# A fused transformer layer on one core: the first branch gated where it is evicted, a shift moved to DVE, a copy that scales, and scalar operands in a search

## The chip, the cores and the metric

One core of a Trainium2 chip runs the whole layer as one program. The metric is the device time of an execution in microseconds (us); a kernel's time is the median of its runs. The profile is that of one execution. Engines: PE (matrix products), DVE and POOL (elementwise work), ACT (elementwise work, functions and copies), SP (issues most transfers). Each engine runs its own instructions in order and waits on semaphores for the others.

## The reference, cut to what matters

```
hx = rms_norm(x) * (1 + sc1) + sh1                       # 1024 tokens, 1024 features
... projections of hx: recurrence branch xo, attention branch, and two gates xga, xgb (1024 features each)
a  = (rms_norm(xo) * silu(xg)) @ w_branch_a              # first branch
bb = attention_output @ w_branch_b                       # second branch
y  = (sigmoid(xga) * a + sigmoid(xgb) * bb) @ w_out      # merge, output projection
x  = x + g1 * y
h  = rms_norm(x) * (1 + sc2) + sh2                       # second norm
aff = softmax(h @ w_router)                              # 16 experts
gate, idx = top_k(aff.T, 128)                            # each expert takes its 128 best tokens
x  = x + g2 * sum over experts of gate * swiglu(h[idx])
out = rms_norm(x)
```

## The kernel before, in words

Each float32 product is made of three matmuls on parts with shorter mantissas (hi*hi, lo*hi, hi*lo; the helpers mm3 and mm3g, L176 to L178), so whatever becomes an operand of a product is split first: ACT writes the hi part (L92) and DVE the lo part (L93).

The program goes through these stages: normalisation and projections (to about 480 us), the recurrence (to about 640), attention (to about 1021), the merge (to about 1085), the output projection with the second norm and the router (to 1209), a search for the 16 thresholds (to about 1238), sixteen experts (1245 to about 1812) and the final norm.

During the recurrence and attention, matmuls of independent work ("fill") stand between the steps of the dependent chains. Part of it are the gate projections: `gate_proj(i, c)` makes gates i (0 for the first branch, 1 for the second), and each 128x512 block goes from PSUM (`pj`) through ACT into a tile `stg` and by a transfer to the DRAM buffer sGT (`staged`, L66). The last fill, `branch_a` (L873), multiplies the first branch by its weights: 16 blocks of 128x512, each copied by ACT from PSUM into a tile `stg` (a pool of three) and stored in sBA. It ends at 1021 us.

The merge has 16 steps, one for each 128x512 block (L978 to L1012). `gates` is called GA steps ahead: it loads both gate blocks from sGT into tiles `sgm`, ACT takes their sigmoids (L983), it loads the first branch's block from sBA into a tile `ba` and POOL multiplies it by the first gate (L987). The step itself is 12 matmuls of the second branch into PSUM `pb`, then three DVE instructions and one ACT copy: the second gate times `pb` (L1010, tile `sgm`), the sum (L1011, tile `ba`), and the split into the hi and lo parts `mg` (L92, L93).

The output projection (`py`) multiplies `mg` by the weights `wo`/`whi`, `wlo`. For each of 8 token tiles `y_part` adds the residual, takes the mean square, and from the norm's factor r (on POOL) it makes h: DVE multiplies x by r and s2 (L1090), POOL adds sh2 (L1091), and h is stored for the experts' gathers. PE transposes x1 (`pth`), multiplies by the router's weights (`plg`); `router` makes the softmax: DVE and ACT produce the exponentials `re`, DVE their reciprocal sum (L1113) and the affinities `aff` (L1114). `spread` repeats each affinity eight times with an ACT copy (`affb`, L1120), PE transposes that (`psp`, L1122), and two copies (`ar`) follow.

The search fixes the 128th largest affinity of each expert, three bits a round in ten rounds: DVE counts (`junk`, 128x1024, L1200 and L1202), writes a flag (`fl`), PE sums flags (`pn`), and DVE makes the next candidate from the count and an offset `bo`, which is the base plus a constant of its partition (L1214, L1217; both 128x1).

PE's order is fixed by the order in which the code emits it; the other engines' order is made by a scheduler from priorities (`tc.high_priority`). Transfers issued from SP are in one queue, in SP's order.

Of the kernel before, what the change touches and what calls it, by code (L numbers as in the profile page):

```python
# [9 lines left out]
F32 = mybir.dt.float32  # L10
# [18 lines left out]
def view(t, off, dims):  # L29
    """The tile's partitions with free dimensions [stride, size] from element off on."""  # L30
    a = t if isinstance(t, bass.AP) else t[:]
    return bass.AP(tensor=a.tensor, offset=a.offset + off, ap=[list(a.ap[0])] + [list(d) for d in dims])
# [13 lines left out]
def _layer(tc, nc, top, A, out):  # L46
# [35 lines left out]
    def rsqrt(pool, ss, n, scale, name):  # L82
        """(ss * scale + eps) ** -0.5"""
# [6 lines left out]
    def split(hi, lo, src, eng=None):  # L90
        """hi: src rounded to the parts' width; lo: what is left (exact)."""
        nc.scalar.copy(hi, src)  # L92
        (eng or nc.vector).tensor_tensor(lo, src, hi.bitcast(F32), op=OP.subtract)  # L93
# [3 lines left out]
    class Fill:  # L97
        """Matmuls of independent work, emitted between the steps of a dependent chain: the time is the tensor engine's."""
# [27 lines left out]
        def flushed(self):  # L126
            """The PSUM bank is on its way out: no matmuls into it for some steps."""
            self.wait = self.pause
# [7 lines left out]
    class Stream:  # L136
        """The weight chunks of the first sub-layer in the order of their use; each is loaded one chunk ahead."""
# [18 lines left out]
    def wload(src, kt, ncols, rowlen, off, hl=None):  # L156
        """A chunk of a weight: kt row tiles of 128, ncols columns from off on; as hi and lo."""
# [14 lines left out]
    def mm3g(p, a, b, nk, first=True, last=True):  # L172
        """p += sum over k of a[k].T @ b[k]; a, b: pairs of functions of k giving the hi and lo parts."""
# [15 lines left out]
    # the tokens, halves of them apart: [half][hi, lo]  # L189
# [15 lines left out]
    def natural(hi, lo, emit, tiles):  # L205
        """Token rows on the partitions: emit(token tile, PSUM); ctx tiles are 0, 1, x tiles 2 to 9."""
# [10 lines left out]
    def transposed(hi, lo, m, emit, ctx, halves=(0, 1)):  # L217
        """Features on the partitions: emit(first token, number of tokens, PSUM)."""
# [23 lines left out]
    with ExitStack() as st:  # L242
# [11 lines left out]
        # token tile t is loaded, normalised and transposed beside these row tiles of w_mod (9: after them)  # L254
# [51 lines left out]
        # rows 0, 1: the products with the hi parts of silu(c), silu(c_ctx); rows 2, 3: with the lo parts  # L306
# [64 lines left out]
    def rope_swap(o, x, s, eng):  # L371
        """o = x with the halves of each axis exchanged, times s; [128, heads, 64] each."""
# [4 lines left out]
    def gain_rows(rows, n):  # L377
        """A head's gains on all partitions, and the same with the halves of each axis exchanged."""
# [8 lines left out]
    lbp = consts.tile([128, 2, 4], F32, name="lbp")  # L387
    lb1 = consts.tile([128, 2, 4], F32, name="lb1")
    with ExitStack() as st:
        pool = st.enter_context(mkpool("right", name="sa", bufs=2))  # L390
        pps = st.enter_context(mkpool(name="saps", bufs=1, space=PSUM))
        # lower bounds: a softmax over the two layers' logits, its first component
# [19 lines left out]
        # keys: norm, rotary embedding; values as they are  # L412
# [63 lines left out]
        # the other adaLN parameters, as one row  # L476
# [33 lines left out]
        # their sums over the partitions, piece j of 512 on row j  # L510
# [20 lines left out]
    with ExitStack() as st:  # L531
# [27 lines left out]
        def gate_proj(i, c, halves=(0, 1)):  # L559
# [3 lines left out]
            for m in range(2):  # L563
                def emit(g, n, p):
                    staged(None, n, sGT[i, 2 * c + m, :, g - CT:g - CT + n], p)
# [7 lines left out]
        for i in range(2):  # L573
            for c in range(4):
                # of the last chunk the first half of the tokens first: it makes room
# [53 lines left out]
        def states(h, K, Z, acc, tt):  # L629
# [17 lines left out]
            def advance(d, i0, cs, kt):  # L647
# [3 lines left out]
                for i, c in enumerate(cs):  # L651
# [4 lines left out]
                    else:  # L656
                        # the state before the next chunk
# [60 lines left out]
    with ExitStack() as st:  # L718
# [131 lines left out]
        def branch_in():  # L850
            """The first half of the tokens makes room for the first branch's input."""
# [21 lines left out]
        def branch_a():  # L873
            for c in range(2):
                (w,), ahead = ws.next()
                ahead()
                for n in range(2):
                    for m in range(4):
                        p = pjt()
                        ts = slice(n * 512, n * 512 + 512)  # L880
                        yield from mm3g(p, (lambda k: w[0][:, k, m * 128:m * 128 + 128], lambda k: w[1][:, k, m * 128:m * 128 + 128]),
                                        (lambda k: BA[n][:, 0, k], lambda k: BA[n][:, 1, k]), 4)
                        staged(None, 512, sBA[4 * c + m, :, ts], p)
# [58 lines left out]
    with ExitStack() as st:  # L942
# [4 lines left out]
        # the router on x1: its weights take the norm's gain and the scale; the shift gives a row  # L947
# [21 lines left out]
        # merged branches: [hi, lo][row tiles 0-3, 4-7][tokens 0-511, 512-1023]  # L969
# [3 lines left out]
        with ExitStack() as st2:  # L973
            pool = st2.enter_context(mkpool("right", name="sg", bufs=1))
            steps = [(c, m, n) for c in range(2) for m in range(4) for n in range(2)]
            SG, GA = {}, 2

            def gates(c, m, n):  # L978
                SG[c, m, n] = []
                for b in range(2):  # L980
                    sgm = pool.tile([128, 512], F32, name="sgm", tag="sgm%d" % b, bufs=3)
                    nc.sync.dma_start(sgm, sGT[b, 4 * c + m, :, n * 512:n * 512 + 512])
                    nc.scalar.activation(sgm, sgm, AF.Sigmoid)  # L983
                    SG[c, m, n].append(sgm)
                x = stg.tile([128, 512], F32, name="ba", tag="stg")
                nc.sync.dma_start(x, sBA[4 * c + m, :, n * 512:n * 512 + 512])
                nc.gpsimd.tensor_tensor(x, x, SG[c, m, n][0], op=OP.mult)  # L987
                SG[c, m, n][0] = x
# [3 lines left out]
            for i, (c, m, n) in enumerate(steps):  # L992
# [17 lines left out]
                nc.vector.tensor_tensor(o[1], o[1], p, op=OP.mult)  # L1010
# [18 lines left out]
        nc.gpsimd.tensor_scalar(of16, offs[:, :4], 2.0 ** -16, None, op0=OP.mult)  # L1029
        iob = epc.tile([128, 128, 8], BF, name="iob")  # L1030
# [34 lines left out]
        def y_part(t, c, nc_):  # L1065
            """x1 = x + g1 * y, quarters c, ... of the columns; their part of the mean square."""
# [428 lines left out]
```

## Time and profile before

| | us |
|---|---|
| median of 3 runs | 1856.06 (1855.23 to 1858.42) |
| span of the profiled execution | 1854.5 |
| PE busy in the span | 1731.6 (93%) |
| DVE busy | 1331.0 (72%) |
| ACT busy | 995.4 (54%) |
| POOL busy | 273.7 (15%) |

The profile gives the span of its execution, from the first to the last instruction, and no time beside it; the median lies 1.6 us above that span. Busy shares are means over stages that have different limits.

### The profile page before, as it was taken

How to read it: one execution, taken by the hardware profiler on the slowest of the kernel's cores; microseconds unless marked ns; L12 is line 12 of the kernel's file. 1: busy time of each engine (PE TensorE's matmuls, PEld its weight loads, DVE VectorE, ACT ScalarE, POOL GpSimd, SP SyncE). 2: the span in 40 equal slices, each digit the busy share in tenths (PEclk: the TensorE clock that was granted, in tenths of full speed). 3: DMA queues.
4: the chain of work that ended last, by engine and by line, in shares of the span. 5: the costliest groups of instructions: out<-in, count | busy, mean ns of one | idle time of the engine just before them, and what ended most of it. 6: DMA issues, size and time to landing. Idle time of an engine off the chain costs nothing. (4 is left out here: it accounts for less than half of the span.)

```text
span 1854.5 us, 26192 instructions
## 1 busy us (share of the span) xinstructions
PE 1731.6 (93%) x9820; PEld 1454.9 (78%) x9820; DVE 1331.0 (72%) x2000; ACT 995.4 (54%) x1632; POOL 273.7 (15%) x241
## 2 busy tenths in 40 slices
PE   5899999999999799999999999939999999999995
PEld 2798887899988678787787788828888888887774
DVE  6656323876766466777875664469999999998897
ACT  6422331322323367777876532227777777777665
POOL 3400001020000201111100332140011001001103
PEclk9899999999999999999999999959999999999998
DMA  8285445353332410101212776459999999999972
GB/s 326 93 309 208 171 140 198 106 174 103 103 117 81 130 43 29 46 29 58 89 51 87 261 262 238 159 187 358 378 379 371 379 379 374 376 379 379 370 261 101
DMA packets 206319, 383.87 MB, mean 207 GB/s; under 512 B 17488, under 2 KB 65568, under 8 KB 202864
## 3 DMA queue, kind: packets, MB, share of 16 engines
q1 hardware_dynamic: 194944, 360.92, 54.4%
q0 software_dynamic: 4832, 19.34, 3.8%
q10 hardware_dynamic: 6416, 1.94, 0.4%
q8 instruction: 77, 1.26, 0.3%
q14 instruction: 50, 0.41, 0.1%
HBM read 323.02 MB, written 59.13 MB: 206 GB/s over the span
## 5 line engine op out<-in xcount | busy, mean ns | idle before, releaser
L93 DVE TENSOR_TENSOR elo<-eraw,ehi 128x1024 fp32r<-128x1024 f32 x378 | 452.2, 1221 | 22.2 <-ACT ehi L92 14.4
L92 ACT CAST ehi<-eraw 128x1024 fp32r<-128x1024 f32 x384 | 383.6, 1047 | 86.6 <-PE pgu L178 48.5
L177 PE MATMUL pgu<-elo,xeT 128*128 128x512 f32 x512 | 203.7, 398 | 2.8 <-DVE elo L93 2.4
L176 PE MATMUL pgu<-ehi,xeT 128*128 128x512 f32 x512 | 204.9, 400 | 0.2 <-ACT xeT L92 0.2
L178 PE MATMUL pgu<-ehi,xeT 128*128 128x512 f32 x512 | 202.4, 395 | 0.0
L176 PE MATMUL pj<-hx,whi 128*128 128x512 f32 x448 | 185.4, 414 | 6.5 <-ACT stg L69 5.3
L178 PE MATMUL pj<-hx,wlo 128*128 128x512 f32 x448 | 175.8, 392 | 0.0
L177 PE MATMUL pj<-hx,whi 128*128 128x512 f32 x448 | 175.5, 392 | 0.0
L795 ACT ACTIVATE p<-s,m,qsc 128x512 f32<-128x512 f32 (+1 forms) x192 | 134.3, 713 | 17.7 <-DVE m L792 17.5
L788 DVE TENSOR_REDUCE m<-s 128x1 f32<-128x512 f32 (+1 forms) x192 | 104.3, 596 | 48.5 <-PE s L786 48.2
L176 PE MATMUL pj<-whi,hx 128*128 128x256 f32 x448 | 130.9, 292 | 3.6 <-DVE stg L541 1.9
L92 ACT CAST pT<-ptp 128x512 fp32r<-128x512 f32 x160 | 92.7, 595 | 71.9 <-PE ptp L804 71.8
L178 PE MATMUL pj<-whi,hx 128*128 128x256 f32 x448 | 128.1, 286 | 1.4 <-DVE hx L93 1.3
L93 DVE TENSOR_TENSOR pT<-ptp,pT 128x512 fp32r<-128x512 f32 x160 | 108.3, 685 | 29.2 <-ACT pT L92 28.5
L177 PE MATMUL pj<-wlo,hx 128*128 128x256 f32 x448 | 127.4, 284 | 0.0
L177 PEld LDWEIGHTS pgu<-elo,xeT 128*128 128x128 f32 x512 | 96.3, 188 | 29.0 <-DVE elo L93 8.0
L176 PEld LDWEIGHTS pgu<-ehi,xeT 128*128 128x128 f32 x512 | 96.9, 189 | 21.8 <-ACT xeT L92 0.5
L178 PEld LDWEIGHTS pgu<-ehi,xeT 128*128 128x128 f32 x512 | 96.2, 188 | 22.6 <-DVE xeT L93 0.4
L1385 POOL DMA_INDIRECT ACC<-ye,idx x15 | 34.7, 2316 | 474.9 <-DVE ye L1384 474.9
L176 PE MATMUL pye<-ehi,hdT 128*128 128x512 f32 x256 | 104.8, 409 | 0.0
L177 PE MATMUL pye<-elo,hdT 128*128 128x512 f32 x256 | 102.1, 399 | 1.2 <-DVE elo L93 1.2
L814 PE MATMUL pv<-pT,vs 128*128 128x512 f32 x320 | 102.2, 403 | 0.9 <-DVE pT L93 0.8
(365 smaller groups left out, 3919.7 us busy)
## 6 DMA issues: line engine op xcount, KB each, us to landing
eraw<-in_w_exp_gate SPq DMA_DIRECT2D x64, 1024.0 KB, 12.0
eraw<-in_w_exp_up SPq DMA_DIRECT2D x64, 1024.0 KB, 11.6
eraw<-in_w_exp_down SPq DMA_DIRECT2D x64, 1024.0 KB, 12.2
wm<-in_w_mod SPq DMA_DIRECT2D x24, 1024.0 KB, 6.9
raw<-in_w_in SPq DMA_DIRECT2D x21, 1024.0 KB, 6.1
sFK<-sg SPq DMA_DIRECT2D x32, 256.0 KB, 2.3
sGT<-stg SPq DMA_DIRECT2D x32, 256.0 KB, 2.1
sgm<-sGT SPq DMA_DIRECT2D x32, 256.0 KB, 3.8
```

The source lines that it names most:

```text
L92: nc.scalar.copy(hi, src)
L93: (eng or nc.vector).tensor_tensor(lo, src, hi.bitcast(F32), op=OP.subtract)
L176: nc.tensor.matmul(p, a[0](k), b[0](k), start=s, stop=False)
L177: nc.tensor.matmul(p, a[0](k), b[1](k), start=False, stop=False)
L178: nc.tensor.matmul(p, a[1](k), b[0](k), start=False, stop=e)
L788: nc.vector.tensor_reduce(m[:, a:a + 1], s, axis=AX.X, op=OP.max)
L795: nc.scalar.activation(p, ss[a], AF.Exp, bias=m[:, 7:8], scale=sc, accum_out=SU[t, g][:, a, h:h + 1])
L814: nc.tensor.matmul(PV[t, g].rearrange("p a b -> p (a b)"), VS[:, g, j], hl[i], start=(j == 0 and i == 0), stop=(j == 9 and i == 1))
L1385: nc.gpsimd.indirect_dma_start(out=ACC, out_offset=bass.IndirectOffsetOnAxis(ap=idx[:, :1], axis=0), in_=ye, in_offset=None, compute_op=OP ...
```

## The change

1. `gate_proj` leaves PSUM through a sigmoid for the first branch's gates, so that sGT[0] holds sigmoids.
2. `branch_a` loads the block of gates into its tile (now `ga`) ahead of the matmuls, and DVE multiplies it by the product out of PSUM (L888 of the new kernel), in place of ACT's copy. sBA then holds the gated first branch.
3. `gates` of the merge loads one gate block, not two, and takes one sigmoid; POOL's multiplication is gone. It is called three steps ahead, not two, half of the `ba` tiles come from a pool of their own, and the DVE multiplication out of PSUM has a higher priority.
4. The second norm's `h + sh2` is on DVE; for the last tile it is emitted after `spread`.
5. The affinities' multiplication by the reciprocal sum is the scale of ACT's `affb` instruction; ACT then copies `aff` out of `affb`.
6. `bo` has one tensor and a scalar from a tile, where it had two tensors; a float32 copy of the offsets, `offf`, is made once on POOL.

The lines that differ besides are comments. The core of the diff:

```
@@ gate_proj
-                    staged(None, n, sGT[i, 2 * c + m, :, g - CT:g - CT + n], p)
+                    staged(None, n, sGT[i, 2 * c + m, :, g - CT:g - CT + n], p,
+                           None if i else lambda o, x: nc.scalar.activation(o, x, AF.Sigmoid))
@@ branch_a
+                        x = stg.tile([128, 512], F32, name="ga", tag="stg")
+                        nc.sync.dma_start(x, sGT[0, 4 * c + m, :, ts])
                         yield from mm3g(p, (lambda k: w[0][:, k, m * 128:m * 128 + 128], lambda k: w[1][:, k, m * 128:m * 128 + 128]),
                                         (lambda k: BA[n][:, 0, k], lambda k: BA[n][:, 1, k]), 4)
-                        staged(None, 512, sBA[4 * c + m, :, ts], p)
+                        with tc.high_priority(offset=SH[0]):
+                            nc.vector.tensor_tensor(x, x, p, op=OP.mult)
+                        nc.sync.dma_start(sBA[4 * c + m, :, ts], x)
@@ merge
-            SG, GA = {}, 2
+            SG, GA, HB = {}, 3, 40
             def gates(c, m, n):
-                SG[c, m, n] = []
-                for b in range(2):
-                    sgm = pool.tile([128, 512], F32, name="sgm", tag="sgm%d" % b, bufs=3)
-                    nc.sync.dma_start(sgm, sGT[b, 4 * c + m, :, n * 512:n * 512 + 512])
-                    nc.scalar.activation(sgm, sgm, AF.Sigmoid)
-                    SG[c, m, n].append(sgm)
-                x = stg.tile([128, 512], F32, name="ba", tag="stg")
+                sgm = pool.tile([128, 512], F32, name="sgm", tag="sgm", bufs=GA + 1)
+                nc.sync.dma_start(sgm, sGT[1, 4 * c + m, :, n * 512:n * 512 + 512])
+                nc.scalar.activation(sgm, sgm, AF.Sigmoid)
+                x = (stg.tile([128, 512], F32, name="ba", tag="stg") if n else
+                     pool.tile([128, 512], F32, name="ba", tag="ba", bufs=2))
                 nc.sync.dma_start(x, sBA[4 * c + m, :, n * 512:n * 512 + 512])
-                nc.gpsimd.tensor_tensor(x, x, SG[c, m, n][0], op=OP.mult)
-                SG[c, m, n][0] = x
+                SG[c, m, n] = x, sgm
...
-                nc.vector.tensor_tensor(o[1], o[1], p, op=OP.mult)
+                with tc.high_priority(offset=HB):
+                    nc.vector.tensor_tensor(o[1], o[1], p, op=OP.mult)
@@ second norm
-                h = pool.tile([128, D], F32, name="h", tag="h", bufs=1)
-                nc.vector.scalar_tensor_tensor(h, x1, r, row["s2"], op0=OP.mult, op1=OP.mult)
-                nc.gpsimd.tensor_tensor(h, h, row["sh2"], op=OP.add)
-                nc.sync.dma_start(H[ts], h)
+                if t < 7:
+                    second_norm(t, x1, r)
+
+        def second_norm(t, x1, r):
+            h = pool.tile([128, D], F32, name="h", tag="h", bufs=1)
+            nc.vector.scalar_tensor_tensor(h, x1, r, row["s2"], op0=OP.mult, op1=OP.mult)
+            nc.vector.tensor_tensor(h, h, row["sh2"], op=OP.add)
+            nc.sync.dma_start(H[t * 128:(t + 1) * 128], h)
@@ router, spread
-                nc.vector.tensor_scalar(aff[:, t], e, m[:, 3:4], None, op0=OP.mult)
+            EM[t] = e, m, x1, r
...
-                nc.scalar.copy(ab, aff[:, t, :, None].to_broadcast([128, 16, 8]))
+                e, m, x1, r = EM.pop(t)
+                nc.scalar.activation(ab, e[:, :, None].to_broadcast([128, 16, 8]), AF.Copy, scale=m[:, 3:4])
...
+                nc.scalar.copy(aff[:, t], ab[:, :, 0])
+            if t == 7:
+                second_norm(t, x1, r)
@@ search
-                        nc.vector.scalar_tensor_tensor(bo, base, 65536.0, offs[:, 4:5], op0=OP.mult, op1=OP.add)
+                        nc.vector.tensor_scalar(bo, base, 65536.0, offf[:, 4:5], op0=OP.mult, op1=OP.add)
...
-                        nc.vector.tensor_tensor(bo, base, (of16 if i < 3 else offs)[:, i + 1:i + 2], op=OP.add)
+                        nc.vector.tensor_scalar(bo, base, (of16 if i < 3 else offf)[:, i + 1:i + 2], None, op0=OP.add)
```

Three places show what moves. The first is DVE at the end of the merge, before; `wlo` is the last but one quarter of the output weights, and `sgm<-sgm,pb` is the multiplication out of PSUM.

```order
L1011 TENSOR_TENSOR ba<-ba,sgm 128x512
L93 TENSOR_TENSOR wlo<-raw,whi 128x2048
L93 TENSOR_TENSOR mg<-ba,mg 128x512
L1010 TENSOR_TENSOR sgm<-sgm,pb 128x512
L1011 TENSOR_TENSOR ba<-ba,sgm 128x512
L93 TENSOR_TENSOR mg<-ba,mg 128x512
```

The same place of DVE after the change:

```order
L1015 TENSOR_TENSOR ba<-ba,sgm 128x512
L93 TENSOR_TENSOR mg<-ba,mg 128x512
L1014 TENSOR_TENSOR sgm<-sgm,pb 128x512
L1015 TENSOR_TENSOR ba<-ba,sgm 128x512
L93 TENSOR_TENSOR wlo<-raw,whi 128x2048
L93 TENSOR_TENSOR mg<-ba,mg 128x512
```

The last multiplication out of PSUM stood behind `wlo` and a split; it now stands ahead of `wlo`.

The second place is DVE at a tile of the output projection (the seventh), before:

```order
L1111 TENSOR_SCALAR rm<-rm 128x1
L1090 SCALAR_TENSOR_TENSOR h<-x_11418,r_11514,s_10481 128x1024
L1113 RECIPROCAL rm<-rm 128x1
L1114 TENSOR_SCALAR aff<-re,rm 128x16
L1123 COPY ar_10443<-psp 128x128
```

The same place after the change:

```order
L1121 TENSOR_SCALAR rm<-rm 128x1
L1100 SCALAR_TENSOR_TENSOR h<-x_11371,r_11467,s_10435 128x1024
L1123 RECIPROCAL rm<-rm 128x1
L1101 TENSOR_TENSOR h<-h,sh_10433 128x1024
L1136 COPY ar_10395<-psp 128x128
```

`aff` is gone from DVE, and the addition of sh2 stands in its place, behind the reciprocal for which ACT waits.

The third place is SP, which issues the transfers, where `branch_a` ends and the merge begins, before:

```order
L868 DMA stg<-sOA 128x128
L70 DMA sBA<-stg 128x512 x4
L982 DMA sgm<-sGT 128x512
L70 DMA sBA<-stg 128x512
L982 DMA sgm<-sGT 128x512 x5
L70 DMA sBA<-stg 128x512 x2
L986 DMA ba<-sBA 128x512 x3
```

The same place after the change:

```order
L884 DMA ga<-sGT 128x512
L889 DMA sBA<-ga 128x512
L986 DMA sgm<-sGT 128x512
L990 DMA ba<-sBA 128x512
L986 DMA sgm<-sGT 128x512
L889 DMA sBA<-ga 128x512
L990 DMA ba<-sBA 128x512
L986 DMA sgm<-sGT 128x512
L889 DMA sBA<-ga 128x512
L990 DMA ba<-sBA 128x512
```

A load of gates now stands between the stores of `branch_a`, and the merge's first loads are three of each kind.

## Rows read from the trace of the kernel before

**Rows 1.** Windows by stage: length, busy time by engine, granted clock, DMA share, GB/s.

```profile
900.00:1021.00 121.00, 118.12 (x648) 96.37 (x647) 82.19 (x183) 89.59 (x204) 2.80 (x3) 1.00 0.22 75
1021.00:1090.00 69.00, 60.34 (x292) 50.71 (x291) 49.92 (x57) 36.46 (x53) 29.04 (x17) 0.93 0.76 252
1090.00:1210.00 120.00, 107.62 (x891) 105.69 (x891) 59.91 (x101) 24.90 (x76) 31.61 (x35) 0.97 0.59 211
1300.00:1500.00 200.00, 200.00 (x944) 162.15 (x943) 191.03 (x213) 150.33 (x168) 22.77 (x11) 1.00 1.05 377
```

**Rows 2.** Waits of PE, 1021 to 1210 us: total, times, longest.

```profile
PE psp L1122 <- ACT affb L1120: 10.1, 5, 2.9
PE py L176 <- DVE sgm L1010: 4.2, 1, 4.2
PE pb L176 <- DVE sgm L1010: 3.4, 1, 3.4
```

**Rows 3.** Timeline of PE in the merge: start, duration, instruction.

```profile
1054.75 0.39 PE L178 MATMUL pb<-br,wlo 128*128 128x512 f32 x1
1058.55 0.51 PE L176 MATMUL pb<-br,whi 128*128 128x512 f32 x1 [3.41 <-DVE sgm L1010]
...
1062.53 0.40 PE L177 MATMUL pb<-br,whi 128*128 128x512 f32 x1
...
1076.19 0.28 PE L176 MATMUL py<-wo,mg 128*128 128x256 f32 x1
...
1080.33 0.28 PE L178 MATMUL py<-whi,mg 128*128 128x256 f32 x1
1084.86 0.58 PE L176 MATMUL py<-wo,mg 128*128 128x256 f32 x1 [4.25 <-DVE sgm L1010]
...
1089.81 0.28 PE L178 MATMUL py<-whi,mg 128*128 128x256 f32 x1
```

**Rows 4.** Timeline of DVE at the end of the merge.

```profile
1080.26 2.28 DVE L93 TENSOR_TENSOR wlo<-raw,whi 128x2048 fp32r<-128x2048 f32 x1
1082.46 1.75 DVE L93 TENSOR_TENSOR mg<-ba,mg 128x512 fp32r<-128x512 f32 x1
```

**Rows 5.** Groups of instructions, 1021 to 1090 us: busy, mean ns.

```profile
L987 POOL TENSOR_TENSOR ba<-ba,sgm 128x512 f32<-128x512 f32 x16 | 28.9, 1813 | 120.8 <-ACT sgm L983 94.6 <-DMA ba<-sBA 26.1
...
L93 DVE TENSOR_TENSOR mg<-ba,mg 128x512 fp32r<-128x512 f32 x16 | 15.7, 991 | 4.7 <-ACT mg L92 4.3
L1011 DVE TENSOR_TENSOR ba<-ba,sgm 128x512 f32<-128x512 f32 x16 | 14.1, 889 | 2.8 <-POOL ba L987 2.7
...
L1010 DVE TENSOR_TENSOR sgm<-sgm,pb 128x512 f32<-128x512 f32 x16 | 10.7, 679 | 11.3 <-PE pb L178 7.2 <-ACT sgm L983 4.1
```

**Rows 6.** Timeline of POOL at the third tile and in the search.

```profile
1122.12 2.38 POOL L1091 TENSOR_TENSOR h<-h,sh 128x1024 f32<-128x1024 f32 x1 [1.40 <-DVE rm L1113]
...
1212.24 14.11 POOL L93 TENSOR_TENSOR elo<-eraw,ehi 128x1024 fp32r<-128x1024 f32 x6 [1.87 <-ACT ehi L92]
```

**Rows 7.** One line's instructions, L1114: shortest, median, longest ns.

```profile
L1114 DVE TENSOR_SCALAR aff<-re,rm x8: 234/1445/2378, 1122.2 to 1206.8; 128x16 f32<-128x16 f32 x8
```

**Rows 8.** Timeline of DVE in the search, where rounds begin with `junk`.

```profile
1209.25 1.28 DVE L1200 TENSOR_SCALAR_CACHE_REDUCE junk<-ar,of 128x1024 bf16<-128x1024 uint16 x1
...
1211.18 1.28 DVE L1200 TENSOR_SCALAR_CACHE_REDUCE junk<-ar,cand 128x1024 bf16<-128x1024 uint16 x1
...
1212.38 2.23 DVE L1217 TENSOR_TENSOR bo<-base,of 128x1 f32<-128x1 f32 x1
...
1219.26 0.14 DVE L1226 TENSOR_SCALAR bs<-base 128x1 f32<-128x1 f32 x1
...
1226.88 1.28 DVE L1202 TENSOR_SCALAR_CACHE_REDUCE junk<-ar,cand 128x1024 bf16<-128x1024 f32 x1
```

**Rows 9.** Groups of instructions of ACT, 900 to 1021 us.

```profile
L69 ACT COPY stg<-pj 128x512 f32<-128x512 f32 x16 | 9.4, 590 | 4.9 <-PE pj L178 4.5
```

**Rows 10.** Timeline of SP's queue at the last experts.

```profile
1763.19 9.86 SPq L1318 DMA_DIRECT2D eraw<-in_w_exp_down  x4
```

More of the change, by code (lines that the diff above doesn't have):

```diff
@@ L1029, in _layer @@
         nc.gpsimd.tensor_scalar(of16, offs[:, :4], 2.0 ** -16, None, op0=OP.mult)
+        offf = epc.tile([128, 10], F32, name="offf")
+        nc.gpsimd.tensor_copy(offf, offs)
         iob = epc.tile([128, 128, 8], BF, name="iob")
@@ L1101, in router @@
         def router(t):
-            _, _, _, hT, r = X1.pop(t)
+            _, x1, _, hT, r = X1.pop(t)
             p = ps.tile([128, 512], F32, name="plg", tag="pth")[:, :16]
@@ L1113, in router @@
                 nc.vector.reciprocal(m[:, 3:4], m[:, 2:3])
-                nc.vector.tensor_scalar(aff[:, t], e, m[:, 3:4], None, op0=OP.mult)
+            EM[t] = e, m, x1, r
+        EM = {}
         def spread(t):
```

## The prediction

> **What bounds the kernel now.** I read the page's busy shares first (PE 93% of the span), then windows cut by stage, then PE's waits in the stages where its share falls, and at those places the timelines of the engines that PE waited for. In attention PE is busy 118.1 of 121 us, in the experts all of 200 [rows 1]: nothing that only saves time on DVE, ACT or POOL can shorten these. In the merge it stands still for 8.7 of 69 us and in the output projection for 12.4 of 120 [rows 1], and it is there, and in the search behind them, that the change can pay. Three waits make up most of it: two on DVE's multiplication out of PSUM, and five on ACT's spread of the affinities [rows 2].
>
> **The merge (parts 1 to 3).** What the two stalls cost, from PE's timeline [rows 3]: at full clock the 35 matmul starts from 1076.19 to 1080.33 lie 0.118 us apart, and those of `pb`, with twice the columns, therefore about 0.236. The first stall is 1058.55 - 1054.75 less 0.24, that is 3.6 us; the eleven starts from 1058.55 to 1062.53 then take 3.98 us in place of 2.6, because after the pause the clock was granted at its lower level for a while (the stage's mean is 0.93 [rows 1]): another 1.4. The second is 1084.86 - 1080.33 less 0.12, that is 4.4 us, and its 23 starts up to 1089.81 take 4.95 us in place of 2.7: another 2.2. Together 11.6 us.
>
> Why DVE is late: 2.28 of `wlo` and 1.75 of a split stand ahead of the last multiplication [rows 4], 4.0 of the 4.4. The change's order puts that multiplication ahead of both. And the split is long: 991 ns on the mean and the sum 889 ns, where the multiplication out of PSUM, with as many elements, takes 679 [rows 5]. These two read two tiles of SBUF while POOL multiplies, and POOL's 16 instructions are 28.9 us long [rows 5]. Without them the 32 DVE instructions should fall to about 0.68 each: 15.7 + 14.1 - 21.8 = 8 us less. DVE's 49.9 us in the 69 [rows 1] become about 42; PE's work there, 60.3 less the 3.6 lost to the lower clock, is 57. DVE then has slack, and PE should bound the stage. The loads are 16 fewer of 48; the `ba` load stays and must still come back from a store, for which POOL waited 26.1 us [rows 5], now with one more step of lead and two more tiles. The bounds are 0 (the stalls come back through late loads) and 11.6; I take 11.6, since neither stall waited on a load at its end. Behind it, the last quarter of the output weights becomes the next thing to be late: its raw tile comes free only when `wlo` is done, which now follows the last block. By the present order of events I estimate a few microseconds of margin.
>
> **The price in attention (part 2).** ACT loses 16 copies of 0.59 us [rows 9]; DVE gains 16 multiplications out of PSUM, by the same operation in the merge 0.679 each [rows 5]: 10.9 us, so that its 82.2 of 121 [rows 1] become 93. That is still under PE. But these multiplications must meet a loaded gate, and they empty the PSUM block that the next fill group needs; behind each of them the maxima and splits of the softmax wait for 0.7 us, and PE for those. Sixteen loads of 256 KB are 35 GB/s beside 75 [rows 1], no load on the transfers; but a tile is held from load to store, where it was held from copy to store, and there are three. Bounds: 0 and 0.5 us for each of the 16, 8 us; I take 1.5. The 16 sigmoids of part 1 in place of copies are off the bound in a stage where PE has fill to do: 0; if uncovered, under 1 us.
>
> **The output projection (parts 4, 5).** `aff`, 128x16, takes 234 ns undisturbed and up to 2378 [rows 7], and the longest starts as POOL starts on h at 1122.12 for 2.38 us [rows 6]: it ends with POOL's instruction. The eight excesses add to 8 x 1.35 - 8 x 0.23, about 9.0 us (1.35 is the mean of the shortest, median and longest, an estimate), and PE waits 10.1 us for what hangs on it [rows 2]. The change takes POOL's instruction and `aff` both out; ACT's `affb` waits for the reciprocal alone. In exchange DVE has eight more additions of 128x1024, 1.3 us each (twice 0.68): 10 us on an engine that is busy for 60 of 120 [rows 1]. In the order shown the addition stands behind the reciprocal, so what it delays is the copy `ar` and the next tile's x. Bounds 3 and 9; I take 6. ACT's eight small copies of `aff` follow the spread and are off the chain. At the last tile the addition, 1.3 us, replaces an `aff` between 0.2 and 2.4: no difference.
>
> **The search (part 6).** Rounds begin at 1209.25, 1211.18 and, six rounds later, at 1226.88 [rows 8]. The first has no `bo` and takes 1.93 us; the six take 15.70, and their `bo` are long (2.23 the first) as POOL runs its six 2.35 us instructions from 1212.24 [rows 6]; 1212.24 + 2.35 = 14.59, and `bo` ends at 14.61. Freed of that, `bo` should cost what `bs` costs, 0.14, and a round 1.93 + 0.14 = 2.07: 6 x 2.07 = 12.4, and 3.3 us are saved. But `aff` is a row against it: it is a TENSOR_SCALAR with one tensor and a scalar from a tile, what `bo` becomes, and it was held by POOL all the same [rows 7]; by that row the gain is 0. For it speak `bs`, a one-tensor 128x1 instruction that took 0.14 while POOL's row of six was under way, and the 128x1024 `junk`, with a scalar from a tile, which takes 1.28 there as it did ahead of POOL [rows 8]. I take 3.3, because 128x1 is the nearer row; ends 0 and 3.3.
>
> The Trainium skill sides with that: VectorE: DVE Perf Modes, section "Mode 2×_2P — use both read ports for one tensor", says that a one-tensor instruction on SBUF takes both read ports only where its outermost non-unit dimension can be split between them; 16 elements can and one can't. By that rule the saving is the 3.3 us, and `aff` was held for its 16 elements. No run so far shows the new `bo`.
>
> **The sum.** 11.6 + 6 + 3.3 - 1.5 = 19.4 us. The profiled span of 1854.5 becomes 1835.1, and with the 1.6 us by which the median lies above that span, 1836.7 (1.05% less). The experts, PE-bound, should simply begin earlier.
>
> **The rivals.**
> - *The search isn't freed.* `aff`'s row decides, and `bo` still ends with POOL's instructions: 1840.
> - *The merge stays late.* The new waits are for `ba` or `sgm` landing, or the last output weights miss their margin. Against: the two long waits ended on DVE [rows 2]. For: POOL's 26.1 us on `ba` loads [rows 5], so a fifth of the lead is gone before anything goes wrong. It gives back some 5 to 9 us: 1841.5 to 1845.5.
> - *The experts' stream takes it back.* Transfers are at a share of 1.05 and 377 GB/s throughout [rows 1]; if the stream of weights, not PE, set the pace and started no earlier, the gain would go and the time would be about 1855. Against: PE is busy 200 of 200 us there, and the last four weight loads are issued from 1763 [rows 10], some 50 us before PE is done at about 1812: the stream is ahead.
> - *Attention pays more than the rest gains.* This one ends slower. At each of the 16 groups the gate load comes late (its tile is freed only by an earlier store, in a queue with the other loads), DVE's multiplication waits, PSUM stays full and PE stops. From 1.3 us a group on (21 us over 16, less the 1.5 counted) all is lost; 1.5 us a group, with the clock lost behind each stop, gives 1859. Against: PE's share there is 98% with an eviction that also waits its turn [rows 1, 9].
>
> **How the numbers follow.** Forecast with its three gains, 1830 to 1841: 0.57. Search not freed: 0.15. Merge late: 0.15. Stream: 0.04. Attention: 0.07. The rest, 0.02, is a larger gain. The likeliest gives 1836.7. The range must leave out no more than 0.2: it reaches down to 1829 (the output projection's 9, nothing lost in attention, 3 more of clock) and up to 1849 (merge late and attention at half its upper bound). About 0.2% (3.7 us) is what a measurement of this kernel can tell from no change. Faster 0.88, same 0.05, slower 0.07.
>
> **What would show it.** PE's waits on `sgm` gone and its clock at the full level through 1040 to 1080; the mean of the split and the sum in the merge near 0.68; no PE wait on `affb` over 1 us; `bo` at 0.14 and rounds of 2.0; in attention PE still at 97% or more. A PE wait for `ga` or for the multiplication out of `pj`, waits for loads in the merge, or a `bo` that ends with POOL's instructions would each make it wrong by the price given.

## The result, and the profile after

The changed kernel takes 1836.66 us (median; 1835.66 to 1841.61), before on the same chip 1856.42; the ratio is 0.9897, with a 95% interval of 0.9885 to 0.9910. (The ratios here and below are not quotients of the medians, and differ from these by up to 0.002.) The profiled span is 1833.9 us, 20.6 less than before's 1854.5.

The windows that were cut in [rows 1], now of the changed kernel (same columns):

```profile
900.00:1021.00 121.00, 116.30 (x629) 93.20 (x629) 91.39 (x196) 79.83 (x186) 2.72 (x3) 1.00 0.30 100
1021.00:1090.00 69.00, 69.00 (x394) 60.55 (x393) 46.37 (x63) 29.28 (x38) 3.27 (x8) 1.00 0.78 263
1090.00:1210.00 120.00, 96.87 (x811) 94.52 (x810) 66.61 (x149) 33.50 (x90) 23.22 (x27) 0.91 0.66 234
```

PE no longer stops in the merge: 69.00 of 69 us at full clock, where it was 60.34 at 0.93. In the first row, attention, it is busy for 1.8 us less: 96% of the row, where it was 98%. The last row can't be set beside before's, because the search now begins within it. For stages that shift, marks in the program serve better than fixed times. These are marks on PE's timeline of the kernel before: a transpose in attention shortly ahead of `branch_a`, the merge's first product, the first transpose of x1, the last spread, the first expert product.

```profile
907.35 0.60 PE L804 MATMUL ptp<-ident,p 128*128 128x128 f32 x4
1021.60 0.39 PE L176 MATMUL pb<-br,whi 128*128 128x512 f32 x1
1106.30 0.60 PE L1098 MATMUL pth<-ident,x 128*128 128x128 f32 x4
1208.41 0.47 PE L1122 MATMUL psp<-ident,affb 128*128 128x128 f32 x1 [2.93 <-ACT affb L1120]
1244.90 0.50 PE L176 MATMUL pgu<-ehi,xeT 128*128 128x512 f32 x1 [0.24 <-ACT xeT L92]
```

The same marks in the changed kernel:

```profile
906.46 0.60 PE L806 MATMUL ptp<-ident,p 128*128 128x128 f32 x4
1024.50 0.39 PE L176 MATMUL pb<-br,whi 128*128 128x512 f32 x1
1095.66 0.60 PE L1108 MATMUL pth<-ident,x 128*128 128x128 f32 x4
1190.31 0.48 PE L1135 MATMUL psp<-ident,affb 128*128 128x128 f32 x1 [2.79 <-ACT affb L1133]
1223.58 0.51 PE L176 MATMUL pgu<-ehi,xeT 128*128 128x512 f32 x1 [0.24 <-ACT xeT L92]
```

Differences of these starts give the stages, for these two kernels and for all those run below (us of the profiled execution; "end" is from the first expert product to the end of the span):

| kernel | to the mark | attention | merge | output projection | search | end | span |
|---|---|---|---|---|---|---|---|
| before | 907.35 | 114.25 | 84.70 | 102.11 | 36.49 | 609.60 | 1854.5 |
| changed | 906.46 | 118.04 | 71.16 | 94.65 | 33.27 | 610.32 | 1833.9 |
| merge_only | 908.41 | 117.99 | 71.58 | 103.89 | 36.63 | 609.60 | 1848.1 |
| norm_only | 906.41 | 114.25 | 84.74 | 94.44 | 36.42 | 609.64 | 1845.9 |
| search_only | 904.92 | 114.25 | 82.48 | 102.13 | 34.00 | 611.92 | 1849.7 |
| bo_pair | 909.58 | 118.02 | 71.16 | 94.91 | 35.62 | 611.81 | 1841.1 |
| pool_h | 909.96 | 118.01 | 75.26 | 92.74 | 33.06 | 610.07 | 1839.1 |
| dve_aff | 906.31 | 118.02 | 71.31 | 97.30 | 34.54 | 612.12 | 1839.6 |
| no_ga_load | 909.86 | 115.61 | 71.27 | 95.53 | 33.29 | 611.94 | 1837.5 |
| act_evict | 904.56 | 118.01 | 71.15 | 95.19 | 33.00 | 610.29 | 1832.2 |
| qt2 | 911.83 | 117.40 | 71.16 | 94.58 | 34.01 | 612.22 | 1841.2 |
| stg4 | 904.47 | 115.76 | 71.16 | 94.40 | 33.02 | 610.39 | 1829.2 |
| pool_h_scalar | 908.81 | 118.02 | 71.16 | 93.29 | 33.06 | 610.26 | 1834.6 |
| all_three | 906.34 | 115.87 | 72.11 | 93.19 | 33.30 | 610.29 | 1831.1 |

The change's 20.6 us are -0.9 to the mark, +3.8 in attention, -13.5 in the merge, -7.5 in the output projection, -3.2 in the search and +0.7 behind it.

In the merge, the groups of DVE that [rows 5] showed with means of 991, 889 and 679 ns (1024 to 1072 us):

```profile
L93 DVE TENSOR_TENSOR mg<-ba,mg 128x512 fp32r<-128x512 f32 x15 | 10.4, 691 | 6.5 <-ACT mg L92 6.1
L1015 DVE TENSOR_TENSOR ba<-ba,sgm 128x512 f32<-128x512 f32 x15 | 10.2, 686 | 0.2
L1014 DVE TENSOR_TENSOR sgm<-sgm,pb 128x512 f32<-128x512 f32 x15 | 10.2, 679 | 0.0
```

With POOL gone, the two that read two tiles of SBUF are as short as the one that reads PSUM, which was 679 ns in both kernels. The end of the merge on DVE, which answers to [rows 4]:

```profile
1072.53 0.68 DVE L1014 TENSOR_TENSOR sgm<-sgm,pb 128x512 f32<-128x512 f32 x1
1073.24 0.69 DVE L1015 TENSOR_TENSOR ba<-ba,sgm 128x512 f32<-128x512 f32 x1
1073.85 2.28 DVE L93 TENSOR_TENSOR wlo<-raw,whi 128x2048 fp32r<-128x2048 f32 x1
```

The last multiplication runs ahead of `wlo`, not behind it. PE's waits on `sgm` [rows 2] have gone; of its waits on `affb`, 10.1 us in five, this is left (waits of PE, 1024 to 1195):

```profile
PE psp L1135 <- ACT affb L1133: 4.2, 3, 2.8
```

In the search, DVE's timeline shows the new `bo`, and further on a candidate made of two integer tiles:

```profile
1194.28 0.21 DVE L1233 TENSOR_SCALAR bo<-base,of 128x1 f32<-128x1 f32 x1
...
1206.64 1.06 DVE L1258 TENSOR_TENSOR cand<-basei,offs 128x1 int32<-128x1 int32 x1
```

and POOL's timeline its six splits, which end at 1193.57 + 14.12 = 1207.69:

```profile
1193.57 14.12 POOL L93 TENSOR_TENSOR elo<-eraw,ehi 128x1024 fp32r<-128x1024 f32 x6 [0.67 <-ACT ehi L92]
```

`bo` took 2.23 at the same place [rows 8] and now takes 0.21; the six rounds are 11.65 us (1193.07 to 1204.72), not 15.70. But the search now comes to the integer candidates before POOL is done. The first of them, at 1206.64, ends at 1207.70 with POOL's last instruction: 0.9 of the 4.05 us saved go back there.

### The profile page after: what moved, and what is told of

The parts are those of the page before. It is cut to its first block, busy times and chain, and to the rows that moved or that the text cites. A ratio compares the mean times of both kernels' runs of the same rounds, so it can differ in the third digit from the quotient of the medians.

```text
span 1833.9 us, 26101 instructions
## 1 busy us (share of the span) xinstructions
PE 1728.6 (94%) x9819; PEld 1451.0 (79%) x9820; DVE 1325.1 (72%) x2016; ACT 981.6 (54%) x1608; POOL 225.1 (12%) x218
## 3 DMA queue, kind: packets, MB, share of 16 engines
q10 hardware_dynamic: 6416, 1.94, 0.4%
## 5 line engine op out<-in xcount | busy, mean ns | idle before, releaser
L177 PE MATMUL pgu<-elo,xeT 128*128 128x512 f32 x512 | 203.5, 397 | 2.8 <-DVE elo L93 2.4
L177 PE MATMUL pj<-hx,whi 128*128 128x512 f32 x448 | 175.9, 393 | 0.0
L177 PE MATMUL pj<-wlo,hx 128*128 128x256 f32 x448 | 127.2, 284 | 0.0
L177 PEld LDWEIGHTS pgu<-elo,xeT 128*128 128x128 f32 x512 | 96.2, 188 | 28.6 <-DVE elo L93 8.1
L177 PE MATMUL pye<-elo,hdT 128*128 128x512 f32 x256 | 102.3, 400 | 1.2 <-DVE elo L93 1.2
L176 PEld LDWEIGHTS pj<-hx,whi 128*128 128x128 f32 x448 | 85.2, 190 | 21.1 <-ACT stg L567 5.1
```

Of the source, the lines that this page charges most:

```text
L176: nc.tensor.matmul(p, a[0](k), b[0](k), start=s, stop=False)
L177: nc.tensor.matmul(p, a[0](k), b[1](k), start=False, stop=False)
```

## The experiments

### Each part alone

The first keeps the new gates, gating and merge, and has the rest as before; against the changed kernel:

```
-            nc.vector.tensor_tensor(h, h, row["sh2"], op=OP.add)
+            nc.gpsimd.tensor_tensor(h, h, row["sh2"], op=OP.add)
-                nc.scalar.activation(ab, e[:, :, None].to_broadcast([128, 16, 8]), AF.Copy, scale=m[:, 3:4])
+                nc.scalar.copy(ab, aff[:, t, :, None].to_broadcast([128, 16, 8]))
...
-                        nc.vector.tensor_scalar(bo, base, (of16 if i < 3 else offf)[:, i + 1:i + 2], None, op0=OP.add)
+                        nc.vector.tensor_tensor(bo, base, (of16 if i < 3 else offs)[:, i + 1:i + 2], op=OP.add)
```

> Parts 1 to 3 alone: the gates, the first branch's gating and the merge as in the changed kernel; second norm, affinities and search as before. Theory of separate stages: the stretch from the first pb matmul to the first pth takes about 71.2 us as in the changed kernel (84.7 before), the end of attention comes 3 to 4 us later relative to its start, and the time is about 1846 (10.5 us less than before). Rival, that the merge's gain needs the addition of sh2 off POOL or is given back behind it: the stretch to the first pth as short, but the output projection longer by 5 us or more than before's 102.1, and the time 1850 or more.

Measured: 1849.47 us, before 1857.41, ratio 0.9957 (0.9942 to 0.9971). Merge and attention are those of the changed kernel; the output projection is 1.8 us longer than before's, less than the 5 the rival asked for. The time is a miss, though: it lies nearer to the rival's 1850 than to the 1846 of the theory. The profiled execution has 1.1 us more than before's ahead of the mark besides the 1.8; it is the stages, not the time, that speak for the theory.

The second keeps the second norm and the scaling copy alone (the diff's hunks on gates, `branch_a`, merge and search undone).

> Parts 4 and 5 alone: sh2 added on DVE, the affinities scaled by ACT; gates, merge and search as before. Theory of separate stages: from the first pth to the last psp about 94.7 us as in the changed kernel (102.1 before), time about 1849 (7.4 less). Rival, that this stage gains only because the merge leaves DVE and the output weights earlier: 99 us or more there, time 1853 or more.

Measured: 1848.04, ratio 0.9957 (0.9944 to 0.9970). The output projection takes 94.44 us behind the old merge, as it does behind the new one: the two gains don't need each other.

The third keeps the search alone (all hunks undone but those with `bo` and `offf`).

> Part 6 alone: bo with one tensor and a scalar; all else as before. Theory: bo takes about 0.2 us, the six rounds 11.7 us in place of 15.7, and because POOL's six instructions then still run when the first candidate made from two integer tiles comes up, 0.9 us is given back there: time about 1853.2 (3.2 less). Rival, that bo was short in the changed kernel because POOL's and DVE's work lay otherwise there: bo still ends with POOL's instructions, time within 1 us of before.

Measured: 1856.32, ratio 1.0001 (0.9990 to 1.0012): no change that could be measured. In its profile `bo` is short, and the first integer candidate is held longer than in the changed kernel:

```profile
1207.75 0.21 DVE L1227 TENSOR_SCALAR bo<-base,of 128x1 f32<-128x1 f32 x1
...
1220.12 1.64 DVE L1252 TENSOR_TENSOR cand<-basei,offs 128x1 int32<-128x1 int32 x1
```

Of the search's 36.49 us, 2.5 are saved. The end is 2.3 us longer in this execution (611.92 for 609.60). The theory on `bo` held and the sum did not: by time alone this part is worth nothing that these runs can show, and the 3.2 us in the changed kernel are a stage's, not a time's. The three ratios of the parts add to 0.85% of gain, the whole has 1.03%; their intervals allow the difference.

One more thing shows here. The code of the merge is before's, yet the merge took 82.48 us for 84.70, and PE's waits on `sgm`, 7.6 us in [rows 2], are 4.8:

```profile
PE pb L176 <- DVE sgm L1011: 3.3, 2, 2.9
PE py L176 <- DVE sgm L1011: 1.5, 1, 1.5
```

So what the old merge costs varies by some 2 us from execution to execution.

### What `bo` escapes

```
-                    bo = pool.tile([128, 1], F32, name="bo", tag="bo", bufs=2)
+                    bo2 = pool.tile([128, 2], F32, name="bo", tag="bo", bufs=2)
+                    bo, bb = bo2[:, :1], base[:, :1].to_broadcast([128, 2])
-                        nc.vector.tensor_scalar(bo, base, (of16 if i < 3 else offf)[:, i + 1:i + 2], None, op0=OP.add)
+                        nc.vector.tensor_scalar(bo2, bb, (of16 if i < 3 else offf)[:, i + 1:i + 2], None, op0=OP.add)
```

> The changed kernel with bo two elements wide (128x2, the base repeated, the second element not used). Theory, that a one-tensor instruction is held by POOL when its elements can be split in two and passes when there is one: bo ends with POOL's instructions again, 0.4 to 2.3 us each, and the time is about 1840 (3 to 4 more than the changed kernel). Rival, that one tensor with a scalar passes beside POOL at any width and aff was held for another reason: bo about 0.2 us, time that of the changed kernel, 1836.7.

Measured: 1838.34, ratio 0.9900 (0.9885 to 0.9915). Groups of DVE in its search:

```profile
L1234 DVE TENSOR_SCALAR bo<-base,of 128x2 f32<-128x2 f32 x2 | 1.9, 970 | 0.0
L1234 DVE TENSOR_SCALAR bo<-base,offf 128x2 f32<-128x2 f32 x3 | 1.8, 603 | 0.0
...
L1231 DVE TENSOR_SCALAR bo<-base,offf 128x2 f32<-128x2 f32 x1 | 0.7, 702 | 0.0
```

The first of them on DVE's timeline, and POOL's six splits on its own:

```profile
1197.65 1.33 DVE L1234 TENSOR_SCALAR bo<-base,of 128x2 f32<-128x2 f32 x1
```

```profile
1196.59 14.11 POOL L93 TENSOR_TENSOR elo<-eraw,ehi 128x1024 fp32r<-128x1024 f32 x6 [0.33 <-ACT ehi L92]
```

One element took 0.21 us six times over; two take 0.60 to 0.97 on the mean beside POOL. Each of POOL's six takes 2.35 us, so they end at 1198.94, 1201.29 and so on; the first `bo` ends at 1198.98, and each of the other five within 0.1 us of such an end. So `bo` is held again as soon as it has two elements. The search is 2.4 us longer than in the changed kernel, not 3 to 4: with the slower rounds, POOL is done when the integer candidates come, and those are no longer held. The difference is within what the times can tell; the row, not the time, decides this.

### Which half of the output projection's change counts

Addition of sh2 on POOL again, and ACT scaling:

```
-                if t < 7:
-                    second_norm(t, x1, r)
+                second_norm(t, x1, r)
...
-            nc.vector.tensor_tensor(h, h, row["sh2"], op=OP.add)
+            nc.gpsimd.tensor_tensor(h, h, row["sh2"], op=OP.add)
```

> The changed kernel with the addition of sh2 back on POOL, ahead of the router at the last tile too; the affinities still scaled by ACT. Theory, that PE waited because aff, a one-tensor instruction of 16 elements on DVE, was held by POOL's addition: without aff the output projection (first pth to last psp) stays near 95 to 97 us, time 1837 to 1839. Rival, that POOL's addition costs as much by lengthening the other DVE instructions with two tensors in SBUF, as x + xin: 99 us or more, time 1841 or more.

Measured: 1839.14, ratio 0.9891 (0.9864 to 0.9917). The output projection is 92.74 us, 1.9 less than in the changed kernel: without `aff` on DVE, POOL's addition does no harm there, and the stage is shorter than with DVE's. (This run also puts the last tile's addition ahead of the router, so engine and place are not told apart at that tile.) The last wait for `affb`, 2.8 us in the changed kernel, is at most 1.8 in this one's stage. The merge, whose instructions stand in the same order as in the changed kernel, is 4.1 us longer this time; waits of PE (1027 to 1104):

```profile
PE py L177 <- DVE wo L93: 1.9, 1, 1.9
```

ACT's timeline there:

```profile
1088.97 1.91 ACT L92 CAST wo<-raw 128x2048 fp32r<-128x2048 f32 x1 [7.88 <-DMA raw<-in_w_out]
```

and the windows with the granted clock:

```profile
1078.00:1088.00 10.00, 10.00 (x87) 10.00 (x87) 4.78 (x5) 2.82 (x3) 2.75 (x7) 1.00 0.44 131
1088.00:1098.00 10.00, 7.97 (x54) 7.58 (x53) 5.98 (x6) 2.63 (x3) 0.00 (x0) 0.84 1.00 377
```

That is the last quarter of the output weights coming too late, 1.9 us of waiting and about as much at the lower clock. In the changed kernel the same tile was ready at 1084.67 + 2.29 = 1086.96, and PE's first matmul that reads it (lo*hi, L177) started at 1087.33:

```profile
1084.67 2.29 DVE L93 TENSOR_TENSOR wo<-raw,wo 128x2048 fp32r<-128x2048 f32 x1 [7.93 <-ACT wo L92]
```

```profile
1087.33 0.28 PE L177 MATMUL py<-wo,mg 128*128 128x256 f32 x1
```

The margin was 0.4 us. The profile of merge_only has the same wait with 0.2 us, and that of all_three with 0.6; their merges are 71.58 and 72.11, for 71.16.

The other half: the addition on DVE, and the affinities as before.

```
+                nc.vector.tensor_scalar(aff[:, t], e, m[:, 3:4], None, op0=OP.mult)
             EM[t] = e, m, x1, r
...
-                nc.scalar.activation(ab, e[:, :, None].to_broadcast([128, 16, 8]), AF.Copy, scale=m[:, 3:4])
+                nc.scalar.copy(ab, aff[:, t, :, None].to_broadcast([128, 16, 8]))
-                nc.scalar.copy(aff[:, t], ab[:, :, 0])
```

> The changed kernel with the affinities scaled on DVE and copied by ACT as before, and the addition of sh2 on DVE. By the same theory aff is then 0.23 us long at all eight tiles, PE waits for affb some 0.3 us a tile longer than in the changed kernel, and the output projection takes 95.5 to 97 us: time 1837.5 to 1839. Rival, that the additional instructions on DVE, now ahead of aff, hold it as long as POOL did: 99 us or more, time 1841 or more.

Measured: 1841.06, ratio 0.9911 (0.9885 to 0.9936). The group of DVE that had a mean of 1.34 us before:

```profile
L1124 DVE TENSOR_SCALAR aff<-re,rm 128x16 f32<-128x16 f32 x8 | 1.9, 232 | 0.2
```

and PE's wait behind it:

```profile
PE psp L1136 <- ACT affb L1134: 6.7, 4, 3.0
```

`aff` is short at all tiles, and the stage is 97.30 us, a little over what was expected: at some tiles the addition now stands ahead of `aff`, or of its reciprocal. The time is the one that the rival gave (1841 or more), but the rival's hold on `aff` isn't there, and the stage is short of its 99. So either half takes the hold away; the scaling on ACT alone does it for 9.4 us (102.11 to 92.74), the addition on DVE alone for 4.8.

### What the gating costs in attention

Without the gates' loads, the eviction still on DVE:

```
-                        nc.sync.dma_start(x, sGT[0, 4 * c + m, :, ts])
...
-                            nc.vector.tensor_tensor(x, x, p, op=OP.mult)
+                            nc.vector.tensor_copy(x, p)
```

> The changed kernel with the first branch's blocks copied out of PSUM by DVE, without a load of the gates and without their multiplication (the first branch goes ungated). The changed kernel loses 3.8 us between about 907 and 1016. Theory A, that DVE's 16 evictions delay the splits and maxima of the softmax for which PE waits: attention (first s to first pb) stays 3 to 4 us longer than before's 380 and the time is that of the changed kernel. Theory B, that the loads of the gates and the tiles that they hold are late: attention is back at 380 to 381 and the time is 1833 to 1834.

With the loads, the eviction on ACT:

```
-                            nc.vector.tensor_tensor(x, x, p, op=OP.mult)
+                            nc.scalar.copy(x, p)
```

> The changed kernel with the first branch's blocks copied out of PSUM by ACT, into tiles for which the gates are still loaded but not used (the first branch goes ungated). Theory A (DVE's evictions): attention back at 380 to 381 us, time 1833 to 1834. Theory B (loads and tiles): attention stays 3 to 4 us longer than before's, time that of the changed kernel.

Measured: 1838.35 (0.9892, 0.9866 to 0.9918) and 1836.94 (0.9903, 0.9872 to 0.9935), too wide to tell them apart, and neither is the 1833 to 1834 that one of them should have been; the times forecast for them left out that attention begins at another time in each execution. The stretch from the mark does tell: 114.25 before, 118.04 in the changed kernel, 115.61 without the loads, 118.01 with the loads and ACT's copy. Without the loads 2.4 of the 3.8 us go (theory B), and the 1.4 that stay belong to DVE's evictions (theory A), since before, with ACT's copies and no loads, has none of them; DVE's copy is as long as its multiplication, 0.69 us. But beside the loads it makes no difference which engine empties PSUM: the two prices don't add, and taking the evictions off DVE alone gives nothing back. Which wait the loads bring, ACT's waits in the changed kernel show (905 to 1026 us):

```profile
ACT br L92 <- DMA stg<-sOA: 3.0, 3, 1.9
```

The same row, with the same numbers, stands in the kernel with ACT's copies, and none in the kernel before or in the one without loads: a `ga` holds one of the three `stg` tiles from its load on, the attention output's loads into the same pool come later, and ACT waits for them with the softmax's copies queued behind. A fourth tile needed space, taken from the tiles `qT`; first that alone:

```
-                QT[t, g] = pool.tile([128, 4, 128], F32R, name="qT", tag="qT", bufs=3)
+                QT[t, g] = pool.tile([128, 4, 128], F32R, name="qT", tag="qT", bufs=2)
```

> The changed kernel with two tiles qT in attention in place of three, a control for the next one, which needs their space. Expected: the loss between the matmuls at about 907 and the first pb as in the changed kernel, 3.8 us (within 0.7), if the third tile isn't needed; more if it is.

Then with the fourth tile:

```
-    stg = sgx.enter_context(mkpool(name="stg", bufs=3))
+    stg = sgx.enter_context(mkpool(name="stg", bufs=4))
```

> The same with four tiles stg in place of three. Theory, that a tile ga held from its load on delays the loads of the attention output into the same pool, for which ACT waits with the softmax's work behind it: ACT's wait for stg<-sOA (3.0 us in the changed kernel between 905 and 1026) goes, and the loss from about 907 to the first pb falls from 3.8 to the 1.4 that remained without the gates' loads. Rival, that the queue of transfers or the gates' loads themselves are late: the loss stays at 3 us or more.

Measured, one execution each: 1842.94 and 1830.96. The stretch is 117.40 and 115.76. Two `qT` alone take 0.6 us off the loss, at the edge of what was allowed for, and ACT's wait for `stg<-sOA` is 1.5 us there; with four tiles `stg` that wait has gone, and the loss falls by another 1.6, to 1.5 us. The 12 us between these two single times are not the tile's: 7.4 of them lie ahead of the mark, where both run the same instructions but for those tiles.

### Together

The addition on POOL, and the last integer candidates with a scalar:

```
-                    nc.vector.tensor_tensor(cand, basei, offs[:, i + 1:i + 2], op=OP.bitwise_or)
+                    nc.vector.tensor_scalar(cand, basei, offs[:, i + 1:i + 2], None, op0=OP.bitwise_or)
```

> The changed kernel with sh2 added on POOL again, and the last integer candidates of the search made with one tensor and a scalar. Theory: the output projection takes 92.7 us as with sh2 on POOL before (94.7 in the changed kernel), the candidate that was held for 1.06 us takes 0.2 and the search is 0.9 us shorter (32.3 from the last psp to the first pgu, less what POOL's later addition costs); the merge is again 71.2 when the last output weights come in time. Time 1833 to 1834, ratio about 0.988. Rival: the longer merge seen with sh2 on POOL (75.3) belongs to it, and the time is 1837 to 1838.

Measured: 1835.97, ratio 0.9886 (0.9867 to 0.9906). The time is 2 us above the theory's. The output projection is 93.29 and the merge 71.16, so the longer merge did not belong to the addition. The search is 33.06, as it was with the addition on POOL and without the scalar, where the candidate took 0.36 us and not the 1.06 of the changed kernel. With the scalar the candidate no longer waits, and POOL's hold moves to the next instruction with two tensors, in the next round:

```profile
1207.62 0.21 DVE L1255 TENSOR_SCALAR cand<-basei,offs 128x1 int32<-128x1 int32 x1
...
1209.80 0.65 DVE L1251 TENSOR_TENSOR basei<-basei,add 128x1 int32<-128x1 int32 x1
```

```profile
1196.32 14.12 POOL L93 TENSOR_TENSOR elo<-eraw,ehi 128x1024 fp32r<-128x1024 f32 x6 [2.09 <-ACT ehi L92]
```

POOL is done at 1196.32 + 14.12 = 1210.44, and `basei` at 1210.45.

With the four `stg` tiles as well:

> Four tiles stg with two qT, sh2 added on POOL, and the last integer candidates with a scalar, together. Theory: the loss from about 907 to the first pb is 1.5 us as with four tiles alone (3.8 in the changed kernel), the output projection 93 us (94.7), the search about 33: some 3.5 us less than the changed kernel, time 1832 to 1833.5, ratio about 0.987. Rival, that the stages give back what the others gain or that the start of attention and the experts vary by as much from run to run: a ratio that can't be told from the changed kernel's 0.9897.

Measured: 1833.62 (1831.84 to 1838.30), ratio 0.9874 (0.9851 to 0.9896). Its three stages came as forecast; the merge (72.11) has the wait of 0.6 us for the weights. It is the lowest median of more than one execution, but its interval overlaps that of the changed kernel, so that it beats the changed one is likely and not shown.

## Why the prediction was right

**The sum.** 1836.7 was forecast and 1836.66 measured. That the time came so close is luck: misses of up to 2.3 us in the stages cancelled in part, the span was 1.2 us shorter than forecast (1833.9 for 1835.1), and the median lies 2.8 us above it, not 1.6. By stage, forecast and measured: merge -11.6 and -13.5; output projection -6 and -7.5; search -3.3 and -3.2; attention +1.5 and +3.8; not forecast, -0.9 ahead of the mark and +0.7 behind the search.

**The merge.** The steps held: POOL's hold on DVE's two-tensor instructions went (991 and 889 ns to 691 and 686), the last multiplication passed `wlo`, PE became the bound. No run separates POOL's absence from the higher priority and the earlier loads, so how the gain divides among these is open. The term is undersized by 1.9: some 0.7 of PE's 8.7 us of idle time lay outside the two stalls, was left out and went too; the rest of the 1.9 I can't assign. Nor is the size one number: the old merge took 82.48 in search_only's execution, 2.2 less than in the one that I priced. The margin of the last output weights was mis-sized the other way: 0.4 us in this run, not a few; another execution of the same order lost 4.1 us there, and two more executions waited for 0.2 and 0.6. So the rival of the late merge was closer than its 0.15 sounds, in the form of the weights and not of the loads of `ba` and `sgm`: the 26.1 us that I counted against the lead were a share of POOL's own idle time, and PE has no wait in the changed kernel's merge.

**Attention.** The term of 1.5 was too small by 2.3, and the sign "PE still at 97% or more" failed (96%). Without the gates' loads DVE's evictions cost about what I took (1.4). What I named and did not price is the tile held from its load on. It is most of the rest: 2.4 go with the loads, 1.6 with a fourth tile, and ACT's wait for `stg<-sOA` with either. The rival that all is lost there was far off: 0.24 us a group, not 1.3.

**The output projection.** The size was right within its bounds, but the step that gave part 4 a share is wrong: the scaling on ACT alone brings more than both together. The price of DVE's additions, which I held to lie beside other work, is 1.4 to 1.9 us (94.65 less 93.29 and 92.74), at least in part at the last tile. There PE's wait before and after is 2.93 and 2.79, as forecast ("no difference"), and it is 1.8 in the run that adds on POOL and ahead of the router. The sign "no PE wait on `affb` over 1 us" contradicts that forecast, and failed there and at one earlier tile (1.2 us).

**The search.** `bo` escaped, as the 128x1 rows spoke and `aff`'s did not; it takes 0.21 us, not 0.14, but off the chain: a round takes 1.94 us, as the one without `bo` did (1.93), and not 2.07. That a faster search would run into POOL's last instruction was not foreseen: 4.05 us were saved and 0.9 given back.

The Trainium skill's rule (VectorE: DVE Perf Modes, section "Mode 2×_2P — use both read ports for one tensor") is that a one-tensor instruction takes both ports only where its outermost non-unit dimension can be split. The trace agrees at both widths, if what takes both ports is what POOL holds: 0.21 us with one element, 0.60 to 0.97 on the mean with two.

**The experts.** PE's pace carried the gain through: the end is 610.32 us for 609.60.

## What to carry to other kernels

In this kernel, while POOL worked, it held DVE's instructions that read SBUF by both of their inputs, and also one-tensor instructions of 2 and 16 elements a partition, though they took their constant as a scalar. The counts `junk`, 128x1024 with an accumulated result, kept their 1.28 us. The multiplication that read one input from PSUM was not held (679 ns in both kernels). Two ways out worked on the chains here: scale on ACT, or, where there is one element a partition, take the constant as a scalar. Look for the next such instruction behind it, since the hold moves there. A tile that is loaded earlier than it is used takes a slot from whatever else shares its pool; ask who waits for that pool, not only whether the load itself is in time. Where executions differ by a few microseconds ahead of the change, compare stretches between marks in the program. In attention these agreed to 0.1 us over runs where the times did not; in the merge they did not (84.70 and 82.48 with the old code, 71.16 and 75.26 with the new), so read a stretch in more than one execution, with its waits.

## What was not expected of the hardware

The stretch of attention is 114.25 us in all three kernels that keep the old `branch_a`, while the time up to its mark varies from 904.92 to 907.35 with the same instructions ahead of it. One place where executions differ is PE's wait for the first queries, between 590 and 660 us, before and in the kernel with the search alone:

```profile
PE s L786 <- DVE qT L770: 4.7, 1, 4.7
```

```profile
PE s L787 <- DVE qT L771: 1.1, 1, 1.1
```

The end, too, comes in steps: 609.6 in three kernels, 610.1 to 610.4 in six and 611.8 to 612.2 in five. Why is open; it is not tied to one edit.
